# A hybrid attention block on one core: the linear-attention queries go by seven products, their values take the place among the plain products, and attention's slots are filled anew

## The chip, the cores and the metric

The kernel runs on one core of a Trainium2 chip. The metric is the device time of one execution in microseconds (us); less is better. The program is compared with itself before and after the change, each run several times on the chip, and one execution of each is also recorded by the profiler.

## The reference, cut to what matters

One layer of a streaming encoder on `h`, 16 meta tokens and 1024 frames of width 1024:

```python
h = h + 0.5 * swiglu(rmsnorm(h), ...)                 # first feed-forward block
u = rmsnorm(h)
(aq, ak, av, gq, gk, gv, gr, g_low, gate_a, gate_b) = split(u @ w_in)
ya = window_sink_attention(aq, ak, av, sinks)         # 8 heads, 2 of keys; chunks of 64 frames
og = gated_linear_attention(gq, gk, gv, log_a)        # 4 heads, keys of 64, values of 128
yb = rmsnorm(og) * silu(gr)
h = h + (sigmoid(gate_a) * (ya @ w_branch_att) + sigmoid(gate_b) * (yb @ w_branch_gla)) @ w_out
h = h + 0.5 * swiglu(rmsnorm(h), ...)                 # second feed-forward block
out = rmsnorm(h)[:, 16:]
```

`w_in` holds all projections side by side. In the code their first columns are called C_AQ, C_AK, C_AV (attention), C_GQ (256 columns of queries), C_GK (256 of keys), C_GV (512 of values), C_GR (512 of output gates), C_GL (low rank), all for linear attention, and C_GA, C_GB (1024 each, the merge gates `gate_a` and `gate_b`). P is 128, so a block of P columns is one tile of outputs.

## The kernel before, in words

**Precision.** Every large product is done in three passes: each operand is split into a rounded high part and the rest (a cast on ACT, a subtraction on DVE, as in L125 and L126 for weights), and hi x hi, hi x lo and lo x hi are added up in PSUM (L96 to L98 in a general product, L929 to L931 in the plain ones). One output tile of 128 x 512 with 1024 rows of input takes 8 x 3 = 24 matmuls with 512 columns each.

**Seven products.** The feed-forward blocks and the merge gates go by a scheme that does a product of 2 x 2 blocks with seven block products in place of eight (class Seven; L454 issues all its matmuls). It needs sums of weights (DVE, L437), of inputs (made once) and of outputs. For a pair of gate columns (2 x 128 columns of the output, 1024 frames) it issues 7 x 12 = 84 matmuls of 512 columns.

**Stages in order.** The first feed-forward block takes the time up to about 710 us. Then come the plain products of linear attention (`together`, from L920, up to about 778 us): keys (two blocks of 128), queries (two blocks), one block of output gates and the low-rank projection, with the second half of the frames being scaled (`scaled`, L805: h times its norm by DVE at L808, high part by ACT, low part `ul` by DVE at L812) while the first half is multiplied. The results go to DRAM: `gk_dram`, `gq_dram`, `gr_dram`. Then the merge-gate stage (L1105, up to about 930 us): eight pairs of columns by seven products in a hand-written order (`manual_schedule`). In its last four pairs pieces of the decay computation (`decay`) are slipped in between the products; they read queries and keys from DRAM and write scaled ones back.

**Attention's projections** follow (`firsts`, 930 to 987 us): keys, values, and the queries in four blocks (`q_units`, one block is two units of 24 matmuls, one per half of the frames). A unit's evacuation (`ev_q`, L1214 and L1215) is a cast on ACT and a subtraction on DVE for each of two groups of heads. The second halves of query blocks 2 and 3 are put off (`held`) to behind the first scores.

**Attention's loop** (987 to 1144 us) has 16 chunks. Chunk c: `turn` transposes its probabilities (PE, L1317, `tp`) and splits them (`ptl` is the low part); `scores` of chunk c + 1 (PE `sp`, then DVE, ACT for the softmax, DVE at L1302 for the last scaling of `p`); `values` for every second chunk; then the list `slots[c]`, products that have nothing to do with this chunk and keep PE busy during the softmax; then `attend` (PE at L1333, `po`; its evacuation by ACT at L1339 and L1340, and DVE at L1343 and L1344 writes over the queries in `qs`). The slots before: values of four heads (eight slots, `ev_tok`: ACT copies the block to `v`, and behind the next block PE transposes it into `vt`, DVE copies that at L911 and a DMA writes it to `gv_dram`), output gates 1 to 3 (six slots), and two slots with two branch units each.

**Branch units** (`branch_units`): 12 matmuls for one 128 x 512 tile of `ya @ w_branch_att`, times the gate `ga` that SP loads from `gates` (L1380), by DVE at L1384, stored back by SP (L1385). The weights are cut once for the four units of a pair of blocks. `fill` is the list of all 16 units; a unit of the second half of the frames needs the output of the last chunk.

**Linear attention** (class Gla, about 1144 to 1202 us): two pairs of heads go through eight steps j in turn; in each half-step PE does `at` (L1483), `go` (L1490, L1493) and `kv` (L1502), ACT squares `go` (L1497), DVE copies it to `o` (L1498) and updates the state. Four units of `fill` go ahead of it, one in each of the steps j = 0, 2, 4 and 6, four behind it. From j = 5 on an output gate (`out_gate`, L1521 to L1528) is worked in. After that come the rest of the branch products, `w_out`, and the second feed-forward block to the end.

**What sets the order.** PSUM has eight banks of 128 x 512, taken in turn from two pools of four (`bank`); `ttile` is a pool of four temporary tiles; raw weights have two tiles in `r_main`, cut weights six in `w_main`. Outside the hand-written stage a scheduler orders the instructions of each engine; SP issues nearly all DMAs, one after the other.

Of the kernel before, what the change touches and what calls it, by code (L numbers as in the profile page):

```python
# [13 lines left out]
AF = mybir.ActivationFunctionType  # L14
# [3 lines left out]
P = 128  # L18
D = 1024
KT = D // P  # L20
# [7 lines left out]
CH_FR = [(0, 512), (512, 512)]  # L28
# [7 lines left out]
def hybrid_kernel(  # L36
# [4 lines left out]
    nc = tc.nc  # L41
# [113 lines left out]
    def raw_tile():  # L155
        return r_main.tile([P, 1024], F32, tag="raw", name="raw")
# [656 lines left out]


    wt = Weights([w_more, w_main, w_main, w_main], [r_main])
    plain_views = [cols_view(w_in, c) for c in (C_GK, C_GK + P, C_GQ, C_GQ + P, C_GR)]
    raws = [wt.raw(v) for v in plain_views[0:2]]
    hw = [None] * 5
    dgs = {}
# [7 lines left out]
    for c in range(2):  # L827
# [3 lines left out]
        for m in range(KT):  # L831
# [4 lines left out]
            n = 0  # L836
# [17 lines left out]
            else:  # L854
# [4 lines left out]
                if m == 4:  # L859
                    ps = double("rep", 3)  # L860
# [24 lines left out]
    def run_late():  # L885
        while late:
            late.pop(0)()

    def ev_keep(dst, scale=None):
        def evac(ps, c0, n):  # L890
            g = ttile("g")
            nc.scalar.activation(g[:, 0:n], ps[:, 0:n], AF.Copy, scale=1.0 if scale is None else scale)
            nc.sync.dma_start(out=dst[:, c0:c0 + n], in_=g[:, 0:n])
        return evac

    def ev_tok(i):

        def evac(ps, c0, n):
# [4 lines left out]
            def turn():  # L903
# [3 lines left out]
                if c0 + n == T:  # L907
# [6 lines left out]
            late.append(turn)  # L914
        return evac

    plain_evac = [ev_keep(gk_dram[0]), ev_keep(gk_dram[1]), ev_keep(gq_dram[0], 0.125), ev_keep(gq_dram[1], 0.125),
                  ev_keep(gr_dram[0])]

    def together(pairs, hooks=()):  # L920

        pss = [(i, c0, n, bank("pj")) for i, (c0, n) in pairs]
        for k in range(KT):
            if k in hooks:
                hooks[k]()
            for i, c0, n, ps in pss:
                wh, wl = [w[k] for w in hw[i]]
                xh, xl = u_hi[k][:, c0:c0 + n], u_lo[k][:, c0:c0 + n]
                nc.tensor.matmul(ps[:, 0:n], wh, xh, start=(k == 0), stop=False)  # L929
                nc.tensor.matmul(ps[:, 0:n], wh, xl, start=False, stop=False)  # L930
                nc.tensor.matmul(ps[:, 0:n], wl, xh, start=False, stop=(k == KT - 1))  # L931
        for i, c0, n, ps in pss:
            plain_evac[i](ps, c0, n)

# [34 lines left out]
    together([(i, ch) for i in range(2) for ch in CH_T[1:]])  # L969
    hw[4] = ktiles(wt.cut(wt.raw(plain_views[4])))  # L970
    low_w = low_weights()
    together([(2, CH_FR[1]), (3, CH_FR[1])])
    ra.close()
    t_r = g7.enter_context(tc.tile_pool(name="tr", bufs=8, side="right"))

# [32 lines left out]
        nc.vector.tensor_sub(lo, b21[k], hi.bitcast(F32))  # L1008
        g8.tops["T4"][k] = (hi, lo)

    def gate_weights(m):

        pair = []
        for i in range(2):
            pair.append(g8.ext_tile() if m % 4 else raw_tile())
            c = C_GA + (m + i) * P
# [4 lines left out]
    def gate_out(m, i, c, x):  # L1021
        if m < KT:
            nc.scalar.activation(x, x, AF.Sigmoid)
        nc.sync.dma_start(out=gates[m + i, :, c * 512:(c + 1) * 512], in_=x)

    def gate_evac(m, i, ps, xs):

# [71 lines left out]
    group, follow = gate_weights(0), gate_weights(2)  # L1099
    made = [group.weights(i) for i in range(AHEAD)]  # L1100
    group.sums(nc.vector)
    manual = tc.manual_schedule(engines={nc.scalar.engine, nc.vector.engine, nc.tensor.engine})
    manual.__enter__()
    for m in range(0, 16, 2):
        others = [decay(*x) for x in pieces.pop(0)] if m >= KT else []  # L1105
        xs = {}
        for i in range(7):
            j = i + AHEAD
            if j < 7:
                made.append(group.weights(j))  # L1110
            elif follow:
# [6 lines left out]
        group, follow = follow, gate_weights(m + 4) if m + 4 < 16 else None  # L1118
    manual.__exit__(None, None, None)
    g7.close()  # L1120
    r1.close()
# [95 lines left out]

    wq = w_in[:, C_AQ:C_AQ + 512].rearrange("(k p) (g i d) -> p k g i d", p=P, g=2, i=4)

    def q_units(i):  # L1220
        views = [(ALLROWS, lambda r, g=g: r.rearrange("p (k g d) -> p k g d", k=KT, g=2)[:, :, g, :], wq[:, :, g, i, :]) for g in range(2)]
        return project_units(views, CH_FR, ev_q(i))

    firsts = [project_units(cols_view(w_in, C_AK), CH_T, ev_k), project_units(cols_view(w_in, C_AV), CH_T, ev_v), q_units(0)]
    for units in firsts:
        units.pop(0)()
    for k in range(4):
# [2 lines left out]
    for units in firsts:  # L1230
        for u in units:
            u()
    held = []
    for i in range(1, 4):
        units = q_units(i)
        units[0]()
        if i < 2:
            units[1]()
        else:
            held.append(units[1])  # L1240

    def values(j):

# [99 lines left out]
            nc.vector.tensor_sub(u[own, 0:256], po[own, cols], qs[0][own, c, :].bitcast(F32))  # L1343
        nc.vector.tensor_add(qs[1][:, c, :], u[:, 0:256], t[:, 0:256])  # L1344

    slots = []
    for i in range(4):
        us = project_units(cols_view(w_in, C_GV + i * P), CH_T, ev_tok(i))
        slots += [us[0:1], us[1:3]]
    for i in range(1, 4):  # L1350
# [8 lines left out]
        def __getitem__(self, i):  # L1359
            return self.v[:, i[1].start // 64:i[1].stop // 64, :]  # L1360

    def branch_units(views, y, m0, load, evac, k=4):
# [12 lines left out]

        return [lambda m=m, c=c: unit(m, *c) for c in CH_FR for m in range(2)]

    def load_a(m, c0, n):
        g = ttile("ga")
# [8 lines left out]
    fill = []  # L1388
    for m0 in range(0, KT, 2):
        views = [(slice(g * 64, g * 64 + 64), lambda r: r.rearrange("p (k m) -> p k m", k=4),  # L1390
                  w_branch_att[g * 256:(g + 1) * 256, m0 * P:(m0 + 2) * P].rearrange("(i d) m -> d i m", d=64)) for g in range(2)]
        fill.append(branch_units(views, ya, m0, load_a, ev_a))
    fill = fill[0][0:2] + fill[1][0:2] + fill[0][2:4] + fill[1][2:4] + fill[2] + fill[3]

    slots += [[fill.pop(0), fill.pop(0)] for _ in range(2)]
    values(0)
    cur = scores(0)
    held[0]()
# [385 lines left out]
```

## Time and profile before

| | |
|---|---|
| runs | 2007.33, 2007.23, 2004.85 us; median 2007.23 |
| profiled execution | 2007.16 us, of which span 2005.5 us |
| granted TensorE clock | 0.998 |
| PE busy (matmul) | 1979.6 us, 11964 instructions |
| DVE, ACT, POOL busy | 1406.9, 895.9, 178.5 us |
| DMA | 343.03 MB, 171 GB/s on average |

How to read the rows of the profile: times are in us from the start of the span. A row of a timeline gives the start, the duration, the engine, the line, the operation, out<-in, the shape, how many alike follow one another (x4), and in brackets how long the engine was idle before, and what ended that idleness. PE is TensorE's matmuls, DVE VectorE, ACT ScalarE, SPq the sequencer of SyncE as it issues DMAs. Lines are those of the kernel before; the changed kernel's are four to six higher from attention's part on.

### The profile page before, as it was taken

What the parts mean: (1) busy time and instruction counts of PE and PEld (TensorE: products, weight loads), DVE (VectorE), ACT (ScalarE), POOL (GpSimd) and SP (SyncE); (2) the same over time, 40 slices, a digit from 0 to 9 for tenths busy, and PEclk for the clock granted to TensorE, in tenths of its full rate; (3) what the DMA queues carried; (4) which work ended last, traced back from release to release, by engine and by line L of the source; (5) the groups of instructions that cost most, each with busy time, mean ns of one, the idle gap of its engine ahead of it and who ended that gap; (6) DMA issues with size and microseconds to landing.
All of it is one profiled execution on the core that took longest, in us unless ns stands there. A gap on an engine that the chain in (4) does not pass through costs nothing.

```text
span 2005.5 us, 31822 instructions
## 1 busy us (share of the span) xinstructions
PE 1979.6 (99%) x11964; PEld 1756.2 (88%) x11964; DVE 1406.9 (70%) x2455; ACT 895.9 (45%) x1756; POOL 178.5 (9%) x214
## 2 busy tenths in 40 slices
PE   8999999999999999999999999999999999999998
PEld 7999999999999988888888878888888888878887
DVE  6976776676778786476466568469767767757786
ACT  5544444443322254465366545345444444442225
POOL 1000000002323000004100000110000000022220
PEclk9999999999999999999999999999999999999999
DMA  6243453349975333356212647741534534699832
GB/s 212 86 149 128 149 180 129 125 147 378 363 278 199 96 128 106 117 178 180 53 54 69 213 146 224 238 148 47 189 126 148 189 126 140 206 362 346 299 106 85
DMA packets 284619, 343.03 MB, mean 171 GB/s; under 512 B 26407, under 2 KB 192033, under 8 KB 284465
## 3 DMA queue, kind: packets, MB, share of 16 engines
q1 hardware_dynamic: 265376, 274.82, 41.6%
q10 hardware_dynamic: 17296, 61.29, 8.1%
q0 software_dynamic: 1792, 4.89, 0.7%
q8 instruction: 94, 1.54, 0.3%
q14 instruction: 61, 0.49, 0.1%
HBM read 220.66 MB, written 120.27 MB: 170 GB/s over the span
## 4 chain that ended last, share of the span: by engine, by line
PE 92%; DVE 3%; DMA 2%; issue 1%; ACT 1%; POOL 0%; SPq 0%; POOLq 0%; ACTq 0%; DVEq 0%
PE pb L454 36%; PE pd L454 18%; PE pa L454 9%; PE pj L96 2%; PE pj L97 2%; PE pj L98 2%; PE wo L96 1%; PE wo L98 1%; PE wo L97 1%; PE br L96 1%; PE br L98 1%; PE br L97 1%; PE pd L841 1%; PE pj L929 1%; PE pj L930 1%
## 5 line engine op out<-in xcount | busy, mean ns | idle before, releaser
L454 PE MATMUL pb<-tt,wop 128*128 128x260 f32 (+1 forms) x2280 | 393.0, 326 | 0.0
L454 PEld LDWEIGHTS pb<-tt,wop 128*128 128x128 f32 x2280 | 339.7, 188 | 35.5
L228 ACT CAST wop<-s 128x512 fp32r<-128x512 f32 x268 | 166.1, 621 | 235.4 <-PE pb L454 97.4
L229 DVE TENSOR_TENSOR wop<-s,wop 128x512 fp32r<-128x512 f32 x268 | 188.8, 707 | 116.2 <-ACT wop L228 115.7
L454 PE MATMUL pb<-tm,wop 128*128 128x260 f32 (+1 forms) x1440 | 236.4, 320 | 8.0 <-DMA tm<-f2mid 3.5
L454 PEld LDWEIGHTS pb<-tm,wop 128*128 128x128 f32 x1440 | 208.2, 189 | 28.5 <-ACT h L396 2.8
L228 ACT CAST wop<-raw 128x512 fp32r<-128x512 f32 x201 | 124.9, 622 | 221.8 <-PE pb L454 113.2
L229 DVE TENSOR_TENSOR wop<-raw,wop 128x512 fp32r<-128x512 f32 x201 | 144.0, 718 | 30.9 <-ACT wop L228 30.7
L454 PE MATMUL pd<-tt,wop 128*128 128x260 f32 (+1 forms) x792 | 138.2, 327 | 0.0
L454 PEld LDWEIGHTS pd<-tt,wop 128*128 128x128 f32 x792 | 118.8, 188 | 13.1
L341 DVE SCALAR_TENSOR_TENSOR h<-pb,h 128x520 f32<-128x520 f32 (+1 forms) x136 | 93.9, 692 | 39.7 <-PE pb L454 37.7
L454 PE MATMUL pd<-tm,wop 128*128 128x260 f32 (+1 forms) x720 | 118.8, 319 | 0.0
L454 PE MATMUL pb<-tb,wop 128*128 128x260 f32 (+1 forms) x696 | 115.3, 319 | 0.7 <-DVE m L742 0.7
L454 PE MATMUL pd<-tb,wop 128*128 128x260 f32 (+1 forms) x696 | 115.1, 319 | 0.0
L454 PE MATMUL pa<-tb,wop 128*128 128x260 f32 (+1 forms) x696 | 115.0, 318 | 0.0
L454 PEld LDWEIGHTS pd<-tm,wop 128*128 128x128 f32 x720 | 104.3, 188 | 9.3
L454 PEld LDWEIGHTS pb<-tb,wop 128*128 128x128 f32 x696 | 100.9, 188 | 10.1 <-ACT vec L87 0.8
L454 PEld LDWEIGHTS pa<-tb,wop 128*128 128x128 f32 x696 | 100.7, 188 | 9.4
L454 PEld LDWEIGHTS pd<-tb,wop 128*128 128x128 f32 x696 | 100.7, 188 | 9.4
L437 DVE TENSOR_TENSOR s<-raw 128x512 f32<-128x512 f32 x92 | 63.2, 687 | 56.1 <-DMA raw<-in_ffn_w_up 52.8
L96 PE MATMUL pj<-uh,whi 128*128 128x512 f32 (+2 forms) x256 | 91.5, 357 | 0.0
L437 POOL TENSOR_TENSOR s<-raw 128x512 f32<-128x512 f32 x28 | 37.8, 1351 | 595.4 <-DMA raw<-in_ffn_w_down 472.5
(418 smaller groups left out, 3888.0 us busy)
## 6 DMA issues: line engine op xcount, KB each, us to landing
tm<-f1mid ACTq DMA_DIRECT2D x56, 520.0 KB, 6.3
tm<-f2mid ACTq DMA_DIRECT2D x56, 512.0 KB, 5.7
raw<-in_ffn_w_gate SPq DMA_DIRECT2D x42, 512.0 KB, 3.9
raw<-in_ffn_w_up SPq DMA_DIRECT2D x42, 512.0 KB, 4.0
raw<-in_ffn_w_down SPq DMA_DIRECT2D x80, 256.0 KB, 5.3
f2mid<-kh SPq DMA_DIRECT2D x70, 256.0 KB, 2.9
f2mid<-kl SPq DMA_DIRECT2D x70, 256.0 KB, 3.1
f1mid<-kh SPq DMA_DIRECT2D x63, 260.0 KB, 2.7
```

The costliest lines, as they stand in the source:

```text
L96: nc.tensor.matmul(ps, wh[k], xh[k], start=(k == 0), stop=False)
L97: nc.tensor.matmul(ps, wh[k], xl[k], start=False, stop=False)
L98: nc.tensor.matmul(ps, wl[k], xh[k], start=False, stop=(k == n - 1))
L228: nc.scalar.copy(x[:, 0:n], src)
L229: nc.vector.tensor_sub(x[:, n:2 * n], src, x[:, 0:n].bitcast(F32))
L341: nc.vector.scalar_tensor_tensor(hm, ps, 0.5, hm, op0=ALU.mult, op1=ALU.add)
L437: (eng.tensor_add if add else eng.tensor_sub)(a[s], a[x], a[y])
L454: nc.tensor.matmul(ps, y, z[:, s0:s0 + sn], start=(first and k == 0 and at == 0), stop=(at == 2 and k == len(cols) - 1), skip_group_check= ...
L841: nc.tensor.matmul(ps, y, x[:, c0 + s0:c0 + s0 + sn], start=(n == 0), stop=(n == 3 * LAST - 1), skip_group_check=True)
L929: nc.tensor.matmul(ps[:, 0:n], wh, xh, start=(k == 0), stop=False)
L930: nc.tensor.matmul(ps[:, 0:n], wh, xl, start=False, stop=False)
```

## The change

1. Among the plain products the queries' two blocks (C_GQ) give their places to the first two blocks of values (C_GV), which are evacuated as the values of the slots are: copied by ACT, and transposed later by PE.
2. The queries become the first of nine pairs in the merge-gate stage (PAIRS). Their outputs are scaled by 0.125 on ACT and go to `gq_dram`.
3. Attention's query blocks 0 and 1 do only the first half of the frames ahead of the loop; the second halves take slots 0 and 1, and their weights are loaded and cut once more.
4. The slots are now: two with queries, four with values (blocks 2 and 3), six with output gates, and four with 2, 2, 2 and 1 branch units. The weights of branch units of blocks 0 to 3 are loaded and cut twice, once for each half of the frames.
5. The order of `fill` puts all units of the first half ahead, and linear attention's steps hold a unit only at j = 4.

```diff
-    plain_views = [cols_view(w_in, c) for c in (C_GK, C_GK + P, C_GQ, C_GQ + P, C_GR)]
+    plain_views = [cols_view(w_in, c) for c in (C_GK, C_GK + P, C_GV, C_GV + P, C_GR)]
...
-    plain_evac = [ev_keep(gk_dram[0]), ev_keep(gk_dram[1]), ev_keep(gq_dram[0], 0.125), ev_keep(gq_dram[1], 0.125),
-                  ev_keep(gr_dram[0])]
+    plain_evac = [ev_keep(gk_dram[0]), ev_keep(gk_dram[1]), ev_tok(0), ev_tok(1), ev_keep(gr_dram[0])]
...
                 nc.tensor.matmul(ps[:, 0:n], wl, xh, start=False, stop=(k == KT - 1))
+        run_late()
         for i, c0, n, ps in pss:
             plain_evac[i](ps, c0, n)
...
-    together([(2, CH_FR[1]), (3, CH_FR[1])])
+    together([(i, ch) for i in (2, 3) for ch in CH_T[1:]])
...
+    PAIRS = [C_GQ] + [C_GA + m * P for m in range(0, 16, 2)]
...
+    def gate_out(at, i, c, x):
+        dst = gates[2 * at - 2 + i] if at else gq_dram[i]
+        if at == 0:
+            nc.scalar.activation(x, x, AF.Copy, scale=0.125)
+        elif at <= 4:
             nc.scalar.activation(x, x, AF.Sigmoid)
-        nc.sync.dma_start(out=gates[m + i, :, c * 512:(c + 1) * 512], in_=x)
+        nc.sync.dma_start(out=dst[:, c * 512:(c + 1) * 512], in_=x)
...
-    for m in range(0, 16, 2):
-        others = [decay(*x) for x in pieces.pop(0)] if m >= KT else []
+    for m in range(len(PAIRS)):
+        others = [decay(*x) for x in pieces.pop(0)] if len(PAIRS) - m <= 4 else []
...
-    def q_units(i):
+    def q_units(i, chunks=CH_FR):
...
-    firsts = [project_units(cols_view(w_in, C_AK), CH_T, ev_k), project_units(cols_view(w_in, C_AV), CH_T, ev_v), q_units(0)]
+    firsts = [project_units(cols_view(w_in, C_AK), CH_T, ev_k), project_units(cols_view(w_in, C_AV), CH_T, ev_v), q_units(0, CH_FR[0:1])]
...
+    q_units(1, CH_FR[0:1])[0]()
     held = []
-    for i in range(1, 4):
+    for i in (2, 3):
...
-    slots = []
-    for i in range(4):
+    slots = [q_units(i, CH_FR[1:2]) for i in range(2)]
+    for i in range(2, 4):
         us = project_units(cols_view(w_in, C_GV + i * P), CH_T, ev_tok(i))
         slots += [us[0:1], us[1:3]]
...
-    fill = fill[0][0:2] + fill[1][0:2] + fill[0][2:4] + fill[1][2:4] + fill[2] + fill[3]
-    slots += [[fill.pop(0), fill.pop(0)] for _ in range(2)]
+    fill = [fill_units(m0, CH_FR[0:1]) for m0 in (0, 2)] + [fill_units(m0) for m0 in (4, 6)]
+    fill = [u for us in fill for u in us[0:2]] + fill[2][2:4] + fill[3][2:4] + [u for m0 in (0, 2) for u in fill_units(m0, CH_FR[1:2])]
+    slots += [[fill.pop(0) for _ in range(n)] for n in (2, 2, 2, 1)]
...
-        if j % 2 == 0 and len(fill) > 4:
+        if j == 4 and len(fill) > 4:
             fill.pop(0)()
```

How the order of DVE's instructions changes in three places. First the plain stage, while the second half of the frames is scaled: `h` is scaled, `ul` is the low part that PE multiplies by. DVE before:

```order
L808 SCALAR_TENSOR_TENSOR h_6304<-h_6304,vec,sums 128x520
L812 TENSOR_TENSOR ul_8386<-h_6027,uh_8378 128x512
L812 TENSOR_TENSOR ul_8386<-h_6027,uh_8378 128x8
L812 TENSOR_TENSOR ul_8387<-h_6029,uh_8379 128x512
L812 TENSOR_TENSOR ul_8387<-h_6029,uh_8379 128x8
```

and of the change:

```order
L808 SCALAR_TENSOR_TENSOR h_6304<-h_6304,vec,sums 128x520
L812 TENSOR_TENSOR ul_8386<-h_6027,uh_8378 128x512
L911 COPY g<-vt 128x512
L812 TENSOR_TENSOR ul_8386<-h_6027,uh_8378 128x8
L812 TENSOR_TENSOR ul_8387<-h_6029,uh_8379 128x512
```

The copy of the first transposed value block (`vt`) has come between the low parts of the first and the second row block.

Second, DVE in attention's slot 1, from the last scaling of one chunk's probabilities (L1302 before, L1306 now) to the next chunk's first row of scores. Before:

```order
L1302 TENSOR_SCALAR p<-p,sm 128x146 x4
L1262 TENSOR_TENSOR vz_10620<-vt,vz_10620 82x2x128
L1343 TENSOR_TENSOR u<-po,qs_10613 64x256 x2
L102 TENSOR_TENSOR ptl<-tp,pth 18x512
L1344 TENSOR_TENSOR qs_10614<-u,t 128x256
L102 TENSOR_TENSOR ptl<-tp,pth 128x512
L1294 ISA p,mx<-sp,bias 128x210
```

and of the change:

```order
L1306 TENSOR_SCALAR p<-p,sm 128x146 x4
L1266 TENSOR_TENSOR vz_10855<-vt,vz_10855 82x2x128
L126 TENSOR_TENSOR wlo<-raw,whi 128x1024
L1221 TENSOR_TENSOR qs_10848<-pj,qs_10848 64x8x64
L1347 TENSOR_TENSOR u<-po,qs_10848 64x256 x2
L1221 TENSOR_TENSOR qs_10849<-pj,qs_10849 64x8x64
L1348 TENSOR_TENSOR qs_10849<-u,t 128x256
L102 TENSOR_TENSOR ptl<-tp,pth 18x512
L102 TENSOR_TENSOR ptl<-tp,pth 128x512
L1298 ISA p,mx<-sp,bias 128x210
```

A cut of weights (`wlo`) and the two conversions of the query block from slot 0 (`qs` from `pj`) have been added, ahead of the low parts of the probabilities.

Third, DVE at the end of attention's loop, where `u` from `po` is the evacuation of chunks 14 and 15, and `ga` the branch units' multiplication by the gates. Before:

```order
L1343 TENSOR_TENSOR u<-po,qs_10613 64x256 x2
L102 TENSOR_TENSOR ptl<-tp,pth 82x512
L1344 TENSOR_TENSOR qs_10614<-u,t 128x256
L102 TENSOR_TENSOR ptl<-tp,pth 128x512
L1384 TENSOR_TENSOR ga<-br,ga 128x512 x2
L1343 TENSOR_TENSOR u<-po,qs_10613 64x256 x2
```

and of the change:

```order
L126 TENSOR_TENSOR wlo<-raw,whi 128x1024
L1388 TENSOR_TENSOR ga<-br,ga 128x512
L1347 TENSOR_TENSOR u<-po,qs_10848 64x256 x2
L102 TENSOR_TENSOR ptl<-tp,pth 82x512
L1348 TENSOR_TENSOR qs_10849<-u,t 128x256
L102 TENSOR_TENSOR ptl<-tp,pth 128x512
L1388 TENSOR_TENSOR ga<-br,ga 128x512
L1347 TENSOR_TENSOR u<-po,qs_10848 64x256 x2
```

One multiplication by `ga` stands between the probabilities' low parts and the last chunk's evacuation where two stood, and a cut of weights has come ahead of chunk 14's.

More of the change, by code (lines that the diff above doesn't have):

```diff
@@ L887, in run_late, with ev_keep @@
             late.pop(0)()
-    def ev_keep(dst, scale=None):
+    def ev_keep(dst):
         def evac(ps, c0, n):
             g = ttile("g")
-            nc.scalar.activation(g[:, 0:n], ps[:, 0:n], AF.Copy, scale=1.0 if scale is None else scale)
+            nc.scalar.copy(g[:, 0:n], ps[:, 0:n])
             nc.sync.dma_start(out=dst[:, c0:c0 + n], in_=g[:, 0:n])
@@ L1009, in hybrid_kernel, with gate_weights @@
         g8.tops["T4"][k] = (hi, lo)
-    def gate_weights(m):
+    PAIRS = [C_GQ] + [C_GA + m * P for m in range(0, 16, 2)]
+    def gate_weights(at):
         pair = []
         for i in range(2):
-            pair.append(g8.ext_tile() if m % 4 else raw_tile())
-            c = C_GA + (m + i) * P
+            pair.append(g8.ext_tile() if at % 2 else raw_tile())
+            c = PAIRS[at] + i * P
             nc.sync.dma_start(out=pair[-1].rearrange("p (k m) -> p k m", k=KT),
@@ L1019, in gate_weights @@
         return Group(g8, *pair)
-    def gate_out(m, i, c, x):
-        if m < KT:
+    def gate_out(at, i, c, x):
[3 more added lines that the diff above has]
+        elif at <= 4:
             nc.scalar.activation(x, x, AF.Sigmoid)
-        nc.sync.dma_start(out=gates[m + i, :, c * 512:(c + 1) * 512], in_=x)
+        nc.sync.dma_start(out=dst[:, c * 512:(c + 1) * 512], in_=x)
     def gate_evac(m, i, ps, xs):
@@ L1098, in hybrid_kernel @@
     g8.ring = [w_main] * 6
-    group, follow = gate_weights(0), gate_weights(2)
+    group, follow = gate_weights(0), gate_weights(1)
     made = [group.weights(i) for i in range(AHEAD)]
@@ L1117, in hybrid_kernel @@
                 next(o, None)
-        group, follow = follow, gate_weights(m + 4) if m + 4 < 16 else None
+        group, follow = follow, gate_weights(m + 2) if m + 2 < len(PAIRS) else None
     manual.__exit__(None, None, None)
@@ L1218, in hybrid_kernel @@
     wq = w_in[:, C_AQ:C_AQ + 512].rearrange("(k p) (g i d) -> p k g i d", p=P, g=2, i=4)
-    def q_units(i):
+    def q_units(i, chunks=CH_FR):
         views = [(ALLROWS, lambda r, g=g: r.rearrange("p (k g d) -> p k g d", k=KT, g=2)[:, :, g, :], wq[:, :, g, i, :]) for g in range(2)]
-        return project_units(views, CH_FR, ev_q(i))
-    firsts = [project_units(cols_view(w_in, C_AK), CH_T, ev_k), project_units(cols_view(w_in, C_AV), CH_T, ev_v), q_units(0)]
+        return project_units(views, chunks, ev_q(i))
+    firsts = [project_units(cols_view(w_in, C_AK), CH_T, ev_k), project_units(cols_view(w_in, C_AV), CH_T, ev_v), q_units(0, CH_FR[0:1])]
     for units in firsts:
@@ L1232, in hybrid_kernel @@
             u()
+    q_units(1, CH_FR[0:1])[0]()
     held = []
-    for i in range(1, 4):
+    for i in (2, 3):
         units = q_units(i)
         units[0]()
[L1237 to L1240, printed above, removed]
+        held.append(units[1])
     def values(j):
@@ L1360, in __getitem__, with branch_units @@
             return self.v[:, i[1].start // 64:i[1].stop // 64, :]
-    def branch_units(views, y, m0, load, evac, k=4):
+    def branch_units(views, y, m0, load, evac, k=4, chunks=CH_FR):
         state = {}
@@ L1374, in unit @@
             evac(ps, m0 + m, c0, n, l)
-        return [lambda m=m, c=c: unit(m, *c) for c in CH_FR for m in range(2)]
+        return [lambda m=m, c=c: unit(m, *c) for c in chunks for m in range(2)]
     def load_a(m, c0, n):
@@ L1387, in hybrid_kernel, with fill_units @@
     ya = [[Frames(q[:, :, i * 64:i * 64 + 64]) for i in range(4)] for q in qs]
-    fill = []
-    for m0 in range(0, KT, 2):
+    def fill_units(m0, chunks=CH_FR):
         views = [(slice(g * 64, g * 64 + 64), lambda r: r.rearrange("p (k m) -> p k m", k=4),
                   w_branch_att[g * 256:(g + 1) * 256, m0 * P:(m0 + 2) * P].rearrange("(i d) m -> d i m", d=64)) for g in range(2)]
-        fill.append(branch_units(views, ya, m0, load_a, ev_a))
-    fill = fill[0][0:2] + fill[1][0:2] + fill[0][2:4] + fill[1][2:4] + fill[2] + fill[3]
-    slots += [[fill.pop(0), fill.pop(0)] for _ in range(2)]
+        return branch_units(views, ya, m0, load_a, ev_a, chunks=chunks)
+    fill = [fill_units(m0, CH_FR[0:1]) for m0 in (0, 2)] + [fill_units(m0) for m0 in (4, 6)]
+    fill = [u for us in fill for u in us[0:2]] + fill[2][2:4] + fill[3][2:4] + [u for m0 in (0, 2) for u in fill_units(m0, CH_FR[1:2])]
+    slots += [[fill.pop(0) for _ in range(n)] for n in (2, 2, 2, 1)]
     values(0)
```

## The prediction

> **What bounds the kernel now.** I read the page's busy shares first, then the chain that ended last, then the waits of PE, and last the timelines of the stretches that the change touches. The profile page:
>
> ```profile
> span 2005.5 us, 31822 instructions
> PE 1979.6 (99%) x11964; PEld 1756.2 (88%) x11964; DVE 1406.9 (70%) x2455; ACT 895.9 (45%) x1756; POOL 178.5 (9%) x214
> ...
> PE 92%; DVE 3%; DMA 2%; issue 1%; ACT 1%; POOL 0%; SPq 0%; POOLq 0%; ACTq 0%; DVEq 0%
> ```
>
> TensorE is busy for 99% of the span and carries 92% of the chain. So the kernel is worth what its matmuls cost, plus the places where PE stands still. PE's waits name them (line, who released it, total us, times, longest):
>
> ```profile
> PE br L96 <- ACT qs L1339: 1.2, 1, 1.2
> ...
> PE tp L1317 <- DVE p L1302: 0.8, 2, 0.6
> ...
> PE at L1483 <- ACT kt L1466: 0.5, 1, 0.5
> ```
>
> These three lie where the change works: the first and third around the start of linear attention, the second in attention's loop. The profiled execution took 2007.16 us, which is the span of 2005.5 and 1.66 around it; it stands 0.07 below the median of the three runs, 2007.23, and inside their 2004.85 to 2007.33. I forecast against 2007.16. A measurement of this kernel can tell about 0.2% from no change, 4 us.
>
> **The change, step by step.** *(a) The matmuls.* Two rows of the chain show the price of a full-width matmul, since two groups of 24 stand one whole pair of the gate stage apart:
>
> ```profile
> 794.50 5.44 PE pb L454 x24
> 813.53 5.44 PE pb L454 x24
> ```
>
> 5.44/24 = 0.2267 us each, and 813.53 - 794.50 = 19.03 = 84 x 0.2267: a pair of columns by seven products is 84 matmuls. The queries as plain products are 2 columns x 2 halves x 8 x 3 = 96 matmuls, 21.76 us. As a ninth pair they are 84, 19.04 us. The difference is -2.72. Everything else on PE only moves: values of two heads from attention's slots to the plain stage, 48 query matmuls (10.88 us) from ahead of attention into slots 0 and 1, three branch units (3 x 12 x 0.2267 = 8.16) from linear attention's steps into slots 12 to 15. [...]
>
> The reading-in of the ninth pair's weights and sums on DVE and ACT repeats what the other eight pairs do in the same 19.03 us, beside PE. Its scaling by 0.125 takes the place of the sigmoid on ACT. Nothing there is costed.
>
> *(b) The plain stage.* Values need PE transposes and a copy on DVE that queries don't. All but the first copy fall behind the second half's scaling, where no one waits for them. The first stands in the middle of that scaling (the order shows it). There PE follows DVE operand by operand; PE's and DVE's timelines, and the same copy's row from attention:
>
> ```profile
> 741.40 0.28 PE L929 MATMUL pj<-uh,whi 128*128 128x256 f32 x1
> 741.60 0.39 PE L930 MATMUL pj<-ul,whi 128*128 128x256 f32 x1
> 741.82 0.28 PE L931 MATMUL pj<-uh,wlo 128*128 128x256 f32 x1
> ```
>
> ```profile
> 740.86 2.12 DVE L812 TENSOR_TENSOR ul<-h,uh 128x512 fp32r<-128x512 f32 x6
> ...
> 1016.34 0.66 DVE L911 COPY g<-vt 128x512 f32<-128x512 f32 x1
> ```
>
> Matmuls 0.12 apart are 0.20 and 0.22 apart at 741.6: PE just meets DVE there. A copy of 0.66 put ahead of the next operand delays it by up to that; the four transposes ahead hold PE back too, so not all of it shows. Bounds 0 and 0.66; I take the middle, +0.33.
>
> *(c) Attention's slots.* In each step PE does the slot's matmuls while DVE and ACT turn scores into probabilities; then the transposes (tp) need them. Starts of tp, from PE's timeline:
>
> ```profile
> 1000.47 0.60 PE L1317 MATMUL tp<-ident,p 128*82 128x128 f32 x4
> ...
> 1008.88 1.24 PE L1317 MATMUL tp<-ident,p 128*18 128x128 f32 x8 [0.61 <-DVE p L1302]
> ...
> 1019.27 0.93 PE L1317 MATMUL tp<-ident,p 128*128 128x128 f32 x7
> ...
> 1118.14 1.37 PE L1317 MATMUL tp<-ident,p 128*82 128x128 f32 x8 [0.16 <-DVE p L1302]
> ```
>
> Slots with 24 wide matmuls (slot 0, and the late ones) sit at the edge: 0.61 and 0.16 of waiting. Slot 1, with 48 half-wide ones, has none. After the change slots 0 and 1 are queries, and their evacuation is heavier than a value block's: two conversions on ACT and two on DVE in series, besides the weights that DVE must cut. Tile qs by operation, and DVE's groups in attention:
>
> ```profile
> L1214 ACT CAST qs<-pj x12: 575/580/582, 967.0 to 998.1; 64x512 fp32r<-64x512 f32 x12
> L1215 DVE TENSOR_TENSOR qs<-pj,qs x12: 684/689/696, 968.2 to 998.7; 64x512 fp32r<-64x512 f32 x12
> ```
>
> ```profile
> L126 DVE TENSOR_TENSOR wlo<-raw,whi 128x1024 fp32r<-128x1024 f32 x6 | 7.3, 1218 | 3.8 <-ACT whi L125 3.8
> ```
>
> In slot 1 that is 1.22 of cutting and 2 x 0.69 of conversion on DVE, ahead of the next softmax. Laying the new order out with these durations from 1008.88, DVE frees the third step's probabilities at about 1018.9, while PE is through at 1018.0 (1019.27 less the 1.27 by which I find the query block shorter: wide matmuls for half-wide ones, and no transposes of values behind them): 0.85 waited. The next step, with the second conversion, gives 1.0. Slots 6 and 7 become short as well (an output-gate block of 24 wide matmuls where a value block with its transposes stood), at the 0.16 of the row each: 0.3. Sum +2.15. Bounds: only those 0.3; or both conversions in full in both slots, 4 x 0.69 = 2.76, and 0.4 (half of the 0.8 waits row) for each short slot, 3.56.
>
> *(d) End of attention.* Timeline of PE after the last chunk:
>
> ```profile
> 1144.39 1.19 PE L96 MATMUL br<-qs,whi 128*128 128x512 f32 x4 [1.21 <-ACT qs L1339]
> ...
> 1159.74 0.49 PE L1483 MATMUL at<-gqm,gkm 64*128 64x128 f32 x2 [0.51 <-ACT kt L1466]
> 1163.46 0.49 PE L1483 MATMUL at<-gqm,gkm 64*128 64x128 f32 x4
> 1165.32 0.49 PE L1483 MATMUL at<-gqm,gkm 64*128 64x128 f32 x4
> ```
>
> Before, the first unit after the loop needs frames 512 to 1023, so the last chunk's output: 1.21 waited. After, a unit of the first half stands there, 12 matmuls (2.7 us) that need nothing new, and the wait goes. The 0.51 at 1159.74 comes from ACT, which was held by the cast of linear attention's branch weights; these move, and I let it go. Late next: the last slot has 12 matmuls for 24, and DVE's cut (1.22) stands ahead of the last probabilities' low parts; I put that at 0.5, between nothing and the 1.22 of the cut. Sum -1.2; bounds -1.7 (nothing new) and -0.5 (only the first goes, 0.7 new).
>
> *(e) Linear attention's steps.* A half-step is 1165.32 - 1163.46 = 1.86 us. Units at j = 0, 2 and 6 gave DVE and ACT 2.7 us each to catch up, and go. The first steps without any (j = 1, 3) show no waiting now. From j = 5 on the out gates load them; ACT and DVE around step 5:
>
> ```profile
> 1188.33 1.28 ACT L1522 ACT_TABLE_LOAD   x1
> 1189.62 0.63 ACT L1522 ACTIVATE g<-a 128x512 f32<-128x512 f32 x1
> 1190.15 0.60 ACT L101 CAST ybh<-a 128x512 fp32r<-128x512 f32 x1
> 1190.66 0.27 ACT L1497 ACTIVATE sq<-go 128x128 f32<-128x128 f32 x1
> ```
>
> ```profile
> 1192.46 0.88 DVE L1498 COPY o<-go 128x128 f32<-128x128 f32 x4
> ```
>
> The squares come after table load, sigmoid and cast, and the copies that release the go banks run at 1192.46 to 1193.3. In before the unit of j = 6 covers that. Without it PE wants banks at about 1192.2 (1190.33 and a half-step): 1.1 at most, and I take +0.9. Bounds 0 and 2.4 (1.1 and a table load of 1.28 that now ends late once more). [...]
>
> **Sum:** -2.72 + 0.33 + 2.15 - 1.2 + 0.9 = -0.54, so 2006.6 us.
>
> **Rivals.** *Faster.* The stalls stay away: (b) 0, (c) 0.3, (d) -1.7, (e) 0, which gives -4.1 and 2003.0. For it: 70% on DVE and 45% on ACT leave room on average. Against: the 0.61 of slot 0 shows that a short slot has none. Chance 0.16.
>
> *Slower.* SP's queue is in order. The gates for slot 15's unit (ga) now stand behind a load of linear attention's branch weights, which waits for a raw buffer until DVE has cut the previous one. DVE multiplies by that ga ahead of the last chunk's output, and the first unit after the loop can't hide a long one. What such a wait is in before, where nothing of PE stood behind it:
>
> ```profile
> 1138.59 2.16 SPq L1380 DMA_DIRECT2D ga<-gates  x2
> ```
>
> ```profile
> 1152.02 0.69 DVE L1384 TENSOR_TENSOR ga<-br,ga 128x512 f32<-128x512 f32 x1 [5.55 <-DMA ga<-gates]
> ```
>
> If the same 5.55 falls there, less the 0.5 already counted, the time is 2006.6 + 5.05 = 2011.6. It decides once ga is issued more than some 2 us after the last transposes (a unit's 2.7 us less 0.69 of multiplying). Against it: the store and the raw buffer ahead of it belong to slot 14, and should be through by then. Chance 0.12.
>
> That the change doesn't do what it says is excluded: the new order holds nine groups of 84 matmuls in the gate stage.
>
> **How the numbers follow.** The forecast has 0.72. All terms at their low ends give -2.72 + 0 + 0.3 - 1.7 + 0 = -4.1, 2003.0; all at their high ends -2.72 + 0.66 + 3.56 - 0.5 + 2.4 = +3.4, 2010.6. They won't all lie at an end, and the slower rival's 0.12 lies outside: I take 2003.0 to 2009.5. More than 4 us faster needs the first rival in full, 0.14 with a share of its chance falling short; more than 4 us slower needs the second, 0.12; within 4 us 0.74.
>
> **What would show it.** Right: nine pairs of 19.03 us; the third and fourth tp wait some 0.9 us each on DVE; no wait of br on ACT's qs after the loop; step 6's go waits on the copies. Wrong: periods of tp under 9.0 in slots 1 and 2 without waits; the multiplication by ga waiting for DMA with PE idle at 1140 to 1150; PE standing in the plain stage near 742 for more than 0.66; half-steps of linear attention over 1.9 us from j = 1 on.

## The result: slower, by half clock and late gates

The changed kernel's median is 2017.97 us (7 runs, 2015.24 to 2027.53), that of the kernel before beside it 2007.33 (7 runs, 2003.41 to 2009.59). The ratio is 1.0069, with a 95% interval of 1.0045 to 1.0093: slower. I forecast 2006.6 and a range of 2003.0 to 2009.5. The seven times lie in two heaps: four from 2015.24 to 2017.97, with a mean granted clock of 0.994 to 0.996, and three from 2025.74 to 2027.53, with 0.990 or 0.991. The profiled execution (2025.74, span 2024.0) is one of the second heap, so its trace shows what the three suffer; what the other four suffer has no trace, and is read from it as the rest. Executions that the comparison leaves out as disturbed are not in any of the numbers below.

The first lines of the changed kernel's page, with the chain that ended last:

```profile
span 2024.0 us, 31857 instructions
PE 1992.6 (98%) x11952; PEld 1764.2 (87%) x11952; DVE 1421.5 (70%) x2471; ACT 904.6 (45%) x1769; POOL 179.2 (9%) x214
...
PE 89%; DMA 5%; DVE 3%; ACT 1%; issue 1%; SPq 0%; POOL 0%; DVEq 0%; ACTq 0%; POOLq 0%
```

PE has 12 matmuls less, as the change says, and yet 13 us more of busy time; DMA's share of the chain went from 2% to 5%. Its waits between 700 and 1300 us:

```profile
PE tp L1321 <- DVE p L1306: 4.5, 5, 2.7
PE wo L96 <- ACT whi L125: 2.1, 1, 2.1
PE go L1496 <- ACT kt L1472: 1.5, 1, 1.5
PE br L96 <- ACT ybh L101: 1.0, 1, 1.0
PE pj L928 <- issue: 0.7, 1, 0.7
PE br L97 <- DVE qs L1348: 0.5, 1, 0.5
```

Before, tp waited 0.8, at for kt 0.5 and br for qs 1.2; the wait of 0.7 on issue was there too. So the waits of this stretch grew by (4.5 - 0.8) + 2.1 + (1.5 - 0.5) + 1.0 + (0.5 - 1.2) = 7.1 us. More busy time with fewer matmuls means slower matmuls, and the granted clock (third column from the right) shows where. PE, DVE and the others in stretches of 5 us:

```profile
1170.00:1175.00 5.00, 3.82 (x35) 2.64 (x33) 1.67 (x8) 2.14 (x3) 0.00 (x0) 1.00 0.90 302
1175.00:1180.00 5.00, 4.70 (x26) 3.29 (x28) 3.61 (x12) 2.62 (x12) 0.00 (x0) 0.68 0.32 111
1180.00:1185.00 5.00, 5.00 (x27) 3.44 (x26) 2.60 (x10) 1.16 (x8) 0.00 (x0) 0.50 0.19 56
...
1195.00:1200.00 5.00, 5.00 (x18) 3.60 (x17) 3.32 (x9) 1.00 (x6) 0.00 (x0) 0.50 0.00 0
1200.00:1205.00 5.00, 5.00 (x37) 3.44 (x36) 2.42 (x9) 1.78 (x6) 0.00 (x0) 0.93 0.14 52
```

PE counts as busy all the time, at a clock of 0.50. In the kernel before, the clock is 1.00 throughout this stretch:

```profile
1150.00:1200.00 50.00, 49.49 (x344) 36.47 (x343) 32.49 (x100) 20.48 (x72) 0.00 (x0) 1.00 0.46 150
```

The half clock holds in linear attention, from its second half-step to the unit at j = 4. PE's timeline:

```profile
1173.33 0.49 PE L1489 MATMUL at<-gqm,gkm 64*128 64x128 f32 x4
1175.30 0.49 PE L1496 MATMUL go<-gv,attb 128*128 128x128 f32 x2 [1.48 <-ACT kt L1472]
...
1180.37 0.80 PE L1489 MATMUL at<-gqm,gkm 64*128 64x128 f32 x4
1183.60 0.80 PE L1489 MATMUL at<-gqm,gkm 64*128 64x128 f32 x4
```

PE waits 1.48 us for ACT's kt copies; 1.5 us after it has gone on, at 1176.80, the clock halves, and a half-step takes 1183.60 - 1180.37 = 3.23 us for 1.86. Six of these cost about 6 x 1.37 = 8.2 us, and the unit behind them runs its first ten matmuls or so at half speed, about 2 us: some 10 us, which is the distance between the two heaps.

The other new wait is that ahead of the last transposes. PE, DVE and SP there:

```profile
1149.91 1.91 PE L1321 MATMUL tp<-ident,p 128*82 128x128 f32 x8 [2.74 <-DVE p L1306]
```

```profile
1148.62 0.69 DVE L1388 TENSOR_TENSOR ga<-br,ga 128x512 f32<-128x512 f32 x1 [5.07 <-DMA ga<-gates]
1149.23 0.17 DVE L1304 RECIPROCAL sm<-sm 128x4 f32<-128x4 f32 x1
1149.43 1.05 DVE L1306 TENSOR_SCALAR p<-p,sm 128x210 f32<-128x210 f32 x4
```

```profile
1139.65 0.89 SPq L1389 DMA_DIRECT2D gates<-ga  x1
1143.31 0.32 SPq L1384 DMA_DIRECT2D ga<-gates  x1
```

DVE stands 5.07 us for a gate block of slot 14, and the softmax's last scaling is queued behind it. SP issues that load only at 1143.31, 2.8 us after it had finished with the store ahead of it; what it waits for is the landing of a store from a `ga` tile.

### The profile page after: what moved, and what is told of

The parts are those of the page before. It is cut to its first block, busy times and chain, and to the rows that moved or that the text cites. A ratio compares the mean times of both kernels' runs of the same rounds, so it can differ in the third digit from the quotient of the medians.

```text
span 2024.0 us, 31857 instructions
## 1 busy us (share of the span) xinstructions
PE 1992.6 (98%) x11952; PEld 1764.2 (87%) x11952; DVE 1421.5 (70%) x2471; ACT 904.6 (45%) x1769; POOL 179.2 (9%) x214
## 4 chain that ended last, share of the span: by engine, by line
PE 89%; DMA 5%; DVE 3%; ACT 1%; issue 1%; SPq 0%; POOL 0%; DVEq 0%; ACTq 0%; POOLq 0%
PE pb L454 36%; PE pd L454 18%; PE pa L454 9%; PE pj L96 2%; PE pj L98 2%; PE pj L97 2%; PE wo L96 1%; PE wo L98 1%; PE wo L97 1%; PE pd L841 1%; DMA gates<-ga 1%; PE pj L928 1%; PE pj L929 1%; PE pj L930 1%; DMA ga<-gates 1%
## 5 line engine op out<-in xcount | busy, mean ns | idle before, releaser
L454 PE MATMUL pb<-tt,wop 128*128 128x260 f32 (+1 forms) x2304 | 398.8, 326 | 0.0
L454 PEld LDWEIGHTS pb<-tt,wop 128*128 128x128 f32 x2304 | 344.2, 188 | 36.5
L229 DVE TENSOR_TENSOR wop<-s,wop 128x512 fp32r<-128x512 f32 x272 | 193.7, 715 | 121.3 <-ACT wop L228 120.8
L125 ACT CAST whi<-raw 128x1024 fp32r<-128x1024 f32 x44 | 46.1, 1048 | 67.5 <-PE wo L97 18.2
```

The source lines that it names most:

```text
L125: nc.scalar.copy(hi[:, 0:cols], raw[:, 0:cols])
L229: nc.vector.tensor_sub(x[:, n:2 * n], src, x[:, 0:n].bitcast(F32))
L454: nc.tensor.matmul(ps, y, z[:, s0:s0 + sn], start=(first and k == 0 and at == 0), stop=(at == 2 and k == len(cols) - 1), skip_group_check= ...
```

## The experiments

Each ran beside the kernel before, in four batches. That kernel's median differs a little from batch to batch, so compare the ratios, which stand with their 95% intervals. I call a half-step without a unit thin: its matmuls have 128 columns, those of a unit 512. Theory: (1) with the units taken out, the steps are so thin that a clock once halved stays halved, and a wait of PE halves it; (2) gates come late to DVE in the last slots; (3) query slots wait for conversions and cuts on DVE, as forecast.

**The units back in the steps.** The changed kernel with one edit:

```diff
-        if j == 4 and len(fill) > 4:
+        if j % 2 == 0 and len(fill) > 1:
```

> The changed kernel, with a branch unit again in steps 0, 2, 4 and 6 of linear attention (taken from the four behind it, one is left there). Theory: a wait of PE halves the granted clock, and the thin matmuls of the unfilled steps never bring it back, which costs about 11 us in the profiled execution (half-steps of 3.24 us for 1.86, and the next 4.5 us at half speed). With dense units in between, the clock is back at 1.0 after the first unit: no executions at 2025 or above, all at 2013 to 2017. Rival: the half clock comes from the waits alone and lasts its time whatever runs: still executions near 2015 and near 2026.

Measured: 2009.40 (2007.13 to 2012.49, 11 runs), ratio 1.0011 [1.0003, 1.0020]. No execution over 2012.5, as the theory has it, and lower than it said: the waits on kt, ybh and whi of the changed kernel are not in this profile either. Its clock in the steps:

```profile
1170.00:1180.00 10.00, 10.00 (x77) 7.25 (x75) 5.63 (x20) 4.04 (x14) 0.00 (x0) 1.00 0.83 274
```

Three units in their places take the loss from 0.69% to 0.11%.

**The same edit alone, in the kernel before.** Only the units of j = 0, 2 and 6 are put behind the steps:

```diff
-        if j % 2 == 0 and len(fill) > 4:
+        if j == 4 and len(fill) > 4:
```

> The kernel before, with units in linear attention's steps only at j = 4 (those of 0, 2 and 6 go behind it), nothing else changed. Theory (the thin steps hold a half clock once a wait has brought it): some or all executions 8 to 12 us slower than before, with half-steps of 3.2 us in the profile of such a one; in the others 2007 to 2009. Rival (thin steps are harmless by themselves; the changed kernel's own waits bring the half clock): 2006 to 2009 in all executions and a granted clock of 1.0 in the steps.

Measured: median 2022.08, ratio 1.0059 [1.0032, 1.0086]; two executions at 2003.97 and 2006.79, six from 2020.95 to 2025.56, with clocks of 0.989 to 0.991. The profiled execution (2022.90), in stretches of 10 us:

```profile
1160.00:1170.00 10.00, 8.20 (x42) 5.50 (x40) 3.76 (x11) 3.42 (x11) 0.00 (x0) 0.62 0.84 282
1170.00:1180.00 10.00, 10.00 (x54) 6.82 (x50) 4.63 (x17) 4.61 (x18) 0.00 (x0) 0.50 0.00 0
1180.00:1190.00 10.00, 10.00 (x49) 6.99 (x50) 4.62 (x18) 3.79 (x16) 0.00 (x0) 0.50 0.08 28
1190.00:1200.00 10.00, 10.00 (x62) 7.20 (x61) 7.30 (x23) 2.91 (x11) 0.00 (x0) 0.84 0.07 26
```

and the wait ahead of it:

```profile
PE at L1483 <- ACT kt L1466: 1.8, 1, 1.8
```

This one line of the change makes the kernel before some 15 us slower in six executions of eight; in the two others it costs nothing. So the half clock needs neither the queries nor the slots nor the late gates of the change.

**Is it the wait, or the thin steps?** In the kernel before, units at j = 0 and 4 only (the wait stays ahead of j = 0, dense work follows at once), or at j = 2 and 4 only (dense work follows two steps later):

```diff
-        if j % 2 == 0 and len(fill) > 4:
+        if j in (0, 4) and len(fill) > 4:
```

> The kernel before, with units in linear attention's steps at j = 0 and 4 only. The unit at j = 0 covers the wait for ACT's kt copies (1.8 us when it was gone), the steps 1 to 3 stay thin. Theory now: two things are needed, a wait of PE that halves the clock and thin steps that keep it; without the wait nothing halves it: 2004 to 2009 in nearly all executions, granted clock 1.0 in the steps. Rival: thin steps alone are too little work for the clock, wherever the wait is: again most executions 2019 to 2025.

```diff
-        if j % 2 == 0 and len(fill) > 4:
+        if j in (2, 4) and len(fill) > 4:
```

> The kernel before, with units at j = 2 and 4 only: the wait for the kt copies stays uncovered, the dense unit comes two steps later. Theory: the wait halves the clock in most executions, and the unit at j = 2 (5.4 us at half speed) brings it back: two steps of 6.5 for 3.7 us and a unit of 5.4 for 2.7, so 7 to 9 us slower in those executions (2014 to 2017) in place of 14 to 18, 2005 to 2009 in the others. Rival (the half clock lasts a fixed time of about 25 us once it has come): as with units only at j = 4, 2019 and more in most executions.

Measured with j = 0: 2007.64 as median, ratio 1.0008 [0.9999, 1.0017], and but one execution over 2011 (2013.36, the profiled one). With j = 2: seven executions from 2003.10 to 2007.71, and four from 2012.01 to 2015.74, ratio 1.0004 [0.9991, 1.0017]; I had expected the slow ones to be most of them. The profiled ones, first j = 0, then j = 2:

```profile
1160.00:1170.00 10.00, 8.82 (x37) 6.06 (x37) 3.40 (x9) 2.50 (x4) 0.00 (x0) 0.68 0.83 279
1170.00:1180.00 10.00, 10.00 (x86) 7.08 (x85) 7.40 (x27) 5.46 (x23) 0.00 (x0) 0.98 0.33 107
```

```profile
1160.00:1170.00 10.00, 9.57 (x50) 6.76 (x50) 4.84 (x16) 4.51 (x13) 0.00 (x0) 0.57 0.72 248
1170.00:1180.00 10.00, 10.00 (x44) 7.02 (x40) 3.51 (x12) 1.25 (x8) 0.00 (x0) 0.58 0.08 28
1180.00:1190.00 10.00, 10.00 (x75) 7.14 (x74) 7.86 (x28) 4.79 (x20) 0.00 (x0) 1.00 0.14 52
```

The half clock ends at the end of the first dense unit: near 1170.4 in the one, just behind it (0.98 is the mean from 1170 to 1180), and at 1178.5 in the other, at its eleventh matmul. It has no fixed length, so that rival falls: by the mean clocks of these stretches it lasts 6.8 us here and 17.0 there, by those of the run before 30.8, and by the clock record of the changed kernel's profile 23.89. It does have a grain here: the two short dips of that record last 3.413 us each, 23.89 is 7 times that, and 6.8, 17.0 and 30.8 are 2, 5 and 9 times that within the 0.2 us that the means leave open. One part of my expectation failed: the unit at j = 0 doesn't cover the wait for kt, which comes ahead of it (1.2 us in that profile); it shortens what follows.

**Tiles of their own for the gates.** In the changed kernel:

```diff
     def load_a(m, c0, n):
-        g = ttile("ga")
+        g = qp.tile([P, 512], F32, tag="ga", name="ga", bufs=3)
```

> The changed kernel, with three tiles of their own for the branch units' gates (ga), which shared four temporary tiles with attention's evacuation. Theory: ga of slot 14's second unit is loaded late because it waits for a tile whose store has not landed; with own tiles DVE's wait of 5.07 us for ga and PE's 2.74 us ahead of the last transposes go, and with them the clock's dip behind it (1.4 us): about 4 us less than the changed kernel, 2012 to 2014 in the executions without the long half clock, 2021 to 2023 in those with it. Rival: the transfers themselves are slow there, since the DMA queues are full from 1140 to 1150 us: DVE still waits 3 us or more for ga, and the time is that of the changed kernel within 1.5 us.

Measured: 2010.51 (11 runs), ratio 1.0022 [1.0010, 1.0034]; ten executions from 2007.48 to 2014.22, one at 2021.37. DVE no longer waits for that gate, but PE still waits 2.5 us ahead of the last transposes. DVE there:

```profile
1147.05 1.23 DVE L126 TENSOR_TENSOR wlo<-raw,whi 128x1024 fp32r<-128x1024 f32 x1 [2.10 <-ACT whi L125]
1148.19 0.16 DVE L1301 TENSOR_SCALAR mx<-mx 128x4 f32<-128x4 f32 x1
```

The next branch weights came late in their place, and the softmax's maximum stands behind their cut. So neither side was right: the gates' tiles were one cause of that wait, and the same stretch has another one ready. What helped the time, in the profiled execution (the fastest, 2007.48), was something else. In this order ACT copies kt in time, PE has no wait there, and eight thin half-steps in a row run at full clock:

```profile
1160.00:1170.00 10.00, 10.00 (x59) 8.10 (x57) 6.07 (x12) 5.31 (x8) 0.00 (x0) 1.00 0.73 232
1170.00:1180.00 10.00, 10.00 (x90) 7.10 (x88) 6.03 (x25) 3.40 (x19) 0.00 (x0) 1.00 0.57 200
1180.00:1190.00 10.00, 10.00 (x76) 7.23 (x72) 7.76 (x26) 5.27 (x20) 0.00 (x0) 1.00 0.00 0
```

Thin steps without a wait keep the full clock here; a wait with thin steps behind it can lose it, in six executions of eight above and in four of eleven. In the profiles the two go together: where PE waited 1.2 us or more for kt (four of them), the clock halved behind it, and where it waited 0.5 or not at all, it didn't. That thin steps hold a half clock is shown by edits in both directions; that the wait brings it rests on these profiles, since no edit took the wait away alone, and the execution at 2021.37 has no trace.

**Both edits.**

> The changed kernel with both: units in steps 0, 2, 4 and 6 of linear attention, and three tiles of their own for ga. Theory: both effects add: 2009 to 2013 in every execution, still 2 to 6 us above the kernel before because of the query slots, the table load and the waits at 1245 and 1267 us. Rival (one cause for both, the clock trips only because of the late gates): no better than ga tiles alone in its executions without the long half clock.

Measured: 2010.52, ratio 1.0019 [1.0010, 1.0028], no better than either one. PE waits 2.37 us ahead of the last transposes, for weights again. The theory that the effects add fell. The rival's number holds, but not its cause: the kernel before lost its clock without these gates.

**A third raw tile.** With the units back in the steps:

```diff
+    wt.rs = [r_main, r_main, qp]
     att = ExitStack()
...
     right.close()
+    wt.rs = [r_main]
```

> The changed kernel with units in steps 0, 2, 4 and 6 and a third tile for raw weights during attention and linear attention. Theory: it is the gates' own tiles and transfers that hold DVE in slot 14, so the wait ahead of the last transposes stays at 2 us or more and the time at 2008 to 2011. Rival: raw weights are what comes late there (with tiles of their own for the gates DVE waited for the cast of weights instead): the wait falls below 1.5 us, time 2005 to 2008.

Measured: 2010.01, ratio 1.0014 [1.0006, 1.0023]. PE waits 1.88 us ahead of the last transposes, DVE 3.33 us for gates. The weights alone are not the cause either: mending one of the two leaves the other.

**The branch slots spread among the output gates.** The units are back in the steps, and:

```diff
-    slots += [[fill.pop(0) for _ in range(n)] for n in (2, 2, 2, 1)]
+    b = [[fill.pop(0) for _ in range(n)] for n in (2, 2, 2, 1)]
+    slots = slots[0:9] + b[0:1] + slots[9:11] + b[1:2] + slots[11:12] + b[2:4]
```

> The changed kernel with units in steps 0, 2, 4 and 6, and with the first three branch slots spread among the output-gate slots (slots 9 and 12 hold branch units, 10, 11 and 13 output gates, 14 and 15 branch units). Theory: the wait ahead of the last transposes (2.9 us) comes from weights, gates and stores of three consecutive branch slots together with the loads for linear attention; with fewer of them in a row it falls below 1 us, and the time to 2005 to 2008. Rival: the loads for linear attention alone fill the queues there, so the wait stays above 2 us and the time at 2008 to 2011.

Measured: 2008.48, ratio 1.0008 [1.0000, 1.0017]. The last transposes don't wait any more. But DVE waits for the last slot's gates ahead of the last chunk's evacuation, which is the place that my slower rival named:

```profile
1154.54 0.69 DVE L1388 TENSOR_TENSOR ga<-br,ga 128x512 f32<-128x512 f32 x1 [4.19 <-DMA ga<-gates]
1155.14 0.85 DVE L1347 TENSOR_TENSOR u<-po,qs 64x256 f32<-64x256 f32 x2
```

PE stands 2.27 us for it. **Spread slots with tiles of their own for the gates** are both mends together:

> The changed kernel with units in steps 0, 2, 4 and 6, branch slots spread among output-gate slots, and three tiles of their own for the gates. Theory: with the first the wait ahead of the last transposes was gone but DVE held the last chunk's evacuation for 4.2 us of waiting for gates (2.3 us on PE); own tiles let these gates be loaded ahead, so neither wait is over 1 us: 2004 to 2007, level with the kernel before or up to 2 us faster. Rival: the transfers are late however they are asked for: 2007 to 2010.

Measured: 2005.66, ratio 0.9996 [0.9988, 1.0005]: level with the kernel before. PE's waits in attention are now the 0.61 ahead of the second transposes, which the kernel before has too, and those of the query slots:

```profile
1031.42 1.39 PE L1321 MATMUL tp<-ident,p 128*128 128x128 f32 x8 [0.69 <-DVE p L1306]
1041.47 0.78 PE L1321 MATMUL tp<-ident,p 128*82 128x128 f32 x3 [0.90 <-DVE p L1306]
```

So the late gates and weights at the end of the loop cost about 3 us (1.0011 with the units alone less 0.9996; each ratio is good to some 2 us), and it took both edits to get them back.

**The query slots at other places.** Units back in the steps, and the two query slots at places 4 and 5:

```diff
+    slots = slots[2:6] + slots[0:2] + slots[6:]
```

> The changed kernel with units in steps 0, 2, 4 and 6, and the two query slots moved from places 0 and 1 to places 4 and 5 (values first). Theory: the waits of 0.85 and 1.06 us ahead of the third and fourth transposes come from the query blocks' conversions and the cuts beside them, so they move along to the seventh and eighth transposes, and the first steps wait only the 0.6 that they waited before. Rival: the first steps wait because attention starts there (masks, values and weights come together): the waits stay at the third and fourth.

Measured: 2009.50, ratio 1.0013 [1.0004, 1.0022], as with the units alone. The third and fourth transposes wait no more, and the seventh do:

```profile
1070.01 1.39 PE L1321 MATMUL tp<-ident,p 128*128 128x128 f32 x6 [1.85 <-DVE p L1306]
```

The first wait moves with the query blocks, as the theory has it. The eighth transposes show no wait: the clock has halved for some 3 us in that stretch (0.97 is the mean from 1050 to 1100), and PE itself is late (a period of 10.50 us where 8.95 is usual). So for the second block the theory isn't shown.

**Cuts taken from DVE.** The kernel with spread slots and own tiles, with the weights of values 2 and 3 cut by GpSimd:

```diff
-        us = project_units(cols_view(w_in, C_GV + i * P), CH_T, ev_tok(i))
+        us = project_units(cols_view(w_in, C_GV + i * P), CH_T, ev_tok(i), nc.gpsimd)
...
-                state["w"] = ktiles(wt.cut(wt.raw(views)))
+                state["w"] = ktiles(wt.cut(wt.raw(views), eng=eng))
```

> The same, with the weights of values 2 and 3 cut by GpSimd in place of DVE (the cut in slot 1 is one of them, that in slot 2 isn't). Theory: without the cut of 1.22 us the third transposes wait less than 0.2 us in place of 0.85, the fourth still about 1: the time falls by about 0.7 us. Rival (the conversions alone set the wait): both waits stay as they are.

Measured: 2005.30, ratio 0.9993 [0.9984, 1.0001]. Waits ahead of the second, third and fourth transposes were 0.61, 0.69 and 0.90; now none, 0.39 and 0.94. So the cut is one part of the wait; the rest stays with the conversions still there, and both sides were half right. The time, 0.3 us off the run before, can't tell the sides apart.

**The last version** also cuts the output gates' weights by GpSimd and leaves two units behind the steps (none at j = 6):

```diff
-        if j % 2 == 0 and len(fill) > 1:
+        if j % 2 == 0 and len(fill) > 2:
...
-        slots += [[u] for u in project_units(cols_view(w_in, C_GR + i * P), CH_FR, ev_keep(gr_dram[i]))]
+        slots += [[u] for u in project_units(cols_view(w_in, C_GR + i * P), CH_FR, ev_keep(gr_dram[i]), nc.gpsimd)]
```

> The run before (branch slots spread, three tiles for the gates, weights of values 2 and 3 cut by GpSimd) with the weights of output gates 1 to 3 cut by GpSimd too, and two units left behind linear attention's steps in place of one (none at j = 6). Theory: the wait ahead of the fourth transposes falls from 1.06 to about 0.5 us, the two waits of ot at 1213 us (0.6 each) shrink, and if step 6 without a unit costs what I forecast (0.9) that eats the half of it: 2003.5 to 2005.5 as median, faster than the kernel before by 0.05 to 0.15 per cent. Rival: the thin steps 5 to 7 bring waits of more than 1 us and the half clock in some executions: a median over 2006 and executions over 2010.

Measured: 2003.21 (2001.87 to 2005.49, 11 runs), ratio 0.9981 [0.9972, 0.9990]: faster than the kernel before by 0.19%, a little more than I forecast. Its waits of PE from 700 to 1300 us are few:

```profile
PE tp L1321 <- DVE p L1306: 1.0, 2, 0.6
PE pj L928 <- issue: 0.7, 1, 0.7
PE pj L98 <- DVE wlo L126: 0.2, 1, 0.2
```

That is about 3 us of gain (2006.08 less 2003.21), near the 2.72 that the twelve matmuls are worth. That it is theirs is not shown: PE also waits 1.3 us less in this stretch than in the kernel before (1.9 for 3.2), and cuts by GpSimd and tiles for the gates were never tried in that kernel.

## Why the prediction was wrong, point by point

- **(a) The matmuls, -2.72: right.** The first and second pair of the changed kernel stand 815.71 - 796.67 = 19.04 us apart, as forecast, and PE has 12 matmuls less:

```profile
796.67 5.44 PE pb L454 x24
815.71 5.44 PE pb L454 x24
```

- **(b) The plain stage, +0.33: near nothing.** The copy stands where the order had it and takes 0.69 us, but the next DVE work starts 0.6 us behind it, PE's transposes take 0.36 in the meantime, and no wait shows:

```profile
736.64 0.69 DVE L911 COPY g<-vt 128x512 f32<-128x512 f32 x1 [0.15 <-PE vt L906]
```

- **(c) The slots, +2.15: right in mechanism, a little too large.** I forecast 0.85 and 1.0 for the third and fourth transposes; with an undisturbed clock they wait 0.69 and 0.90 (the rows of the kernel with spread slots, above), all waits of tp there are 2.2 us for 0.8 before, and moving the query slots moved the first of them. The 0.3 for two more short slots did not come.

- **(d) The end of attention, -1.2: wrong.** The first wait, 1.21, went as forecast; what came late next was priced at 0.5 and is 2.74 ahead of the last transposes and 0.48 behind the loop. I had the mechanism (gates behind slow transfers and stores), but as a rival with 0.12, and only at the last chunk's evacuation; it struck one slot earlier, in slot 14, whose gate waits for a temporary tile that a store hadn't yet released. Spreading the slots with tiles of their own took it away, some 3 us (the ratios above). And that I let the 0.51 at 1159.74 go failed: it is 1.48 in the changed kernel. ACT stood for a transfer there as well. Its row, with the table load that then runs ahead of the kt copies:

```profile
1172.85 1.28 ACT L1528 ACT_TABLE_LOAD   x1 [3.24 <-DMA a<-gr_dram]
1174.14 0.63 ACT L1528 ACTIVATE g<-a 128x512 f32<-128x512 f32 x1
1174.68 1.05 ACT L1472 COPY kt<-kt 128x512 f32<-128x512 f32 x2
```

- **(e) Linear attention's steps, +0.9: the step that failed.** The edit that puts the units back takes the ratio from 1.0069 to 1.0011, so taking them out cost about 0.58%, some 11 us (8.6 by the medians), where I had 0.9 and at most 2.4. I looked for late copies at j = 6; in the last version j = 6 has no unit, and PE has no wait there: that term is nothing. What I left out is that every price assumed the granted clock of before, 1.00 throughout this stretch. I read "the first steps without any (j = 1, 3) show no waiting now" as proof that thin steps are free. In these profiles they are, as long as no long wait comes ahead of them. With one, the clock can halve, and the thin steps did not bring it back (0.50 from 1176.80 up to the unit at 1196.53): about 10 us in three of seven executions, 15 us in six of eight of the kernel before with this one edit. The other four executions, the median's among them, pay for the waits; those for kt, ybh and `w_out` were gone from the profile with the units back, and why these come and go with the units stays open.

The sum of the profiled execution: -2.72; +5.5 of PE's idle time over the whole span (25.9 us before, 31.4 after: 7.1 more of waits in this stretch, less elsewhere); +10 of half clock in the steps; and two short dips of 3.4 us at half clock, at the waits that end at 1029.78 and 1149.91, in which matmuls stand 0.43 us apart for 0.23, about 3 us. Outside the stretch the profile of before has two such dips and the changed kernel's one, -1.6. That is 14.2 of the 18.5 by which the span grew; the rest lies in pieces that I have not followed. For the executions of the first heap there is no trace; by the sum they should have all but the +10, which fits 2015 to 2018. Why the weights of `w_out` come 2.1 us late in the changed kernel's profile and in no other wasn't tried.

## What to carry to other kernels

Filler work in a stretch of thin matmuls is not only cover for waits: here it also brought the clock back after one (to 1.00 at 1200.69, at the tenth matmul of the unit at j = 4). Before taking it out, look for the next wait ahead of the stretch and count what half the clock would cost up to the next dense work. And when a multiplication by a loaded block is queued ahead of a softmax or an evacuation on the same engine, price it by that block's whole way, tile, store, load and transfer, and not by the instruction.

## What was unexpected of the hardware

The granted clock can halve right behind a short wait. In the changed kernel's profile it did so behind a wait of 0.69 us, ahead of the transposes at 1029.78 (third column from the right, in stretches of 1 us):

```profile
1029.00:1030.00 1.00, 0.30 (x3) 0.22 (x2) 0.88 (x4) 1.00 (x3) 0.00 (x0) 1.00 0.00 0
1030.00:1031.00 1.00, 1.00 (x6) 0.80 (x6) 1.00 (x3) 0.99 (x3) 0.00 (x0) 0.51 0.00 0
...
1034.00:1035.00 1.00, 1.00 (x6) 0.83 (x5) 0.97 (x3) 0.29 (x2) 0.00 (x0) 1.00 0.64 192
```

It lasted 3.4 us, with dense matmuls running. The same wait of 0.69, and one of 0.90, left the clock at 1.00 in the profile of the kernel with spread slots and own tiles, and the 1.21 us at 1144.39 did so in the kernel before. So the length of a wait doesn't decide by itself whether the clock halves. The half-clock stretches in linear attention last 2 to 9 times 3.413 us (23.89 by the clock record of the changed kernel's profile; 6.8, 17.0 and 30.8 by mean clocks). The thin half-steps, in which PE counts as busy for 5.00 of 5.00 us, did not end it in 19.7 us (1176.80 to 1196.53), while it ended within a unit of matmuls of 512 columns: at the tenth in the changed kernel (1200.69), and at the eleventh with units at j = 2 and 4 (1178.5). What decides whether the clock halves, and when it comes back, can't be seen from these runs.
